# Hybrid decoder step on one core: the first products by two tiles side by side in each chunk, sums of squares and root of x in PSUM

## The chip, the cores and the metric

The kernel runs on one core of a Trainium2 chip. The metric is the device time of one execution in microseconds, the median over several runs. The core has a matrix engine (TensorE; PE, with PEld for its weight loads), VectorE (DVE), ScalarE (ACT), GpSimd (POOL) and a queue, SP, that issues the transfers. Each engine works through its own instructions in the order in which the program issues them.

## The reference, cut to what matters

```
h = RMSNorm(x)                      # x: 1024 prompt + 8 decode rows, 1024 features
parts = h @ w_in                    # q, k, v of 3 dilated groups and one window group, two SiLU gates z, two merge gates g
y = x + W_out( sig(g_A) * (DilAttn(h) * silu(z_A)) @ P_A + sig(g_B) * (SWA(h) * silu(z_B)) @ P_B )
```

All is float32. A product in full precision is made of three products of rounded halves (hi and lo parts): hi by hi, hi by lo and lo by hi. The change lies in how x is normalised and in the first four of the 82 weight tiles, which belong to the merge gates g.

## The kernel before

The 1032 rows lie along the free dimension in three chunks of 344 columns; the 1024 features are eight tiles of 128 (index k). A weight tile is 1024 by 128. `dense_ops` lists the 24 matmuls of a weight tile and a chunk: for each k the products wh·hi, wh·lo, wl·hi. The tiles follow each other in the fixed list `ORDER`, and from tile 4 on a loop (`slot`) issues them, three chunks each, with the attention work of other engines hung between the parts of a slot. The order is written out by hand and nothing moves it.

The opening, lines 1281 to 1345, does tiles 0 to 3 (ga0, gb0, ga1, gb1) while x and the first weights arrive. Chunk 0 is multiplied unnormalised (`h_raw`: hi on ScalarE, line 202, lo on VectorE, line 203); its products are kept (`ev_raw`) and multiplied by the root later (`scale`, line 1267, on GpSimd). Chunks 1 and 2 are normalised first. `squares(j)` squares the eight tiles of chunk j on ScalarE (line 206) and sums them on VectorE into two running sums in SBUF (lines 210 and 212). `h_root(j)` sums over partitions with one float32 matmul (line 216), then takes three ScalarE steps (`rsqrt_act`) and two VectorE steps (lines 241 and 246); the root goes to an SBUF tile `roots[j]`. `h_scale(j, k)` multiplies x by gain and root on VectorE (line 226), rounds hi on ScalarE (line 227) and takes lo = x − hi on GpSimd, for k of 1 and 5 on VectorE (line 232). Later chunk 0 too is scaled so (`scales(0)`), over its raw hi and lo, for tile 4 on.

`w_conv(n)` splits a weight tile: hi on ScalarE (line 137), lo by one GpSimd instruction over all eight k (line 138; tile 0 in two halves). `mm(n, ch, i0, root)` issues 24 matmuls of one tile and, ahead of the one numbered `i0`, `h_root(root)`. Tiles 0 and 1 have PSUM tag "d" (2 buffers), tiles 2 and 3 tag "o" (3); the roots' matmuls have tag "w" (3). `conv_consts` converts small constants on VectorE (lines 1231 to 1236) between the first two and the last six k of `scales(0)`.

Of the kernel before, what the change touches and what calls it, by code (L numbers as in the profile page):

```python
# [10 lines left out]
F32 = mybir.dt.float32  # L11
# [3 lines left out]
ALU = mybir.AluOpType  # L15
# [4 lines left out]
D = 1024  # L20
# [3 lines left out]
KK = D // 128  # L24
CH = 344
# [10 lines left out]
def tile_order():  # L36

    g = [(k, 0, d) for d in range(8) for k in ("ga", "gb")]

    def gates(n):  # L40
        return [g.pop(0) for _ in range(n)]

    GB, GA = (2, 1, 2, 1), ((0, 1, 1), (0, 0, 1), (0, 0, 1), (0, 0, 1))
    o = gates(4) + [("k", 3, 0), ("v", 3, 0), ("q", 3, 0)]
    for c in range(4):
        o += gates(GB[c])
        if c < 3:
            o += [("q", 3, c + 1)]
    for c in range(4):
        for x in range(3):  # L50
            o += [("q", x, c), ("k", x, c), ("v", x, c)] + gates(GA[c][x])
    o += gates(len(g))
    o += [("zb", 0, c) for c in range(4)]
    o += [("za", 0, c) for c in range(4)]
    o += [("br", 0, d) for d in range(8)]
    o += [("out", 0, d) for d in range(8)]
    return o


ORDER = tile_order()  # L60
# [11 lines left out]
def hybrid_step(ctx: ExitStack, tc: tile.TileContext, a):  # L72
    nc = tc.nc
# [11 lines left out]
    def psum(tag, bufs, dt=F32, name=None):  # L85
        return ps.tile([128, 512], dt, tag=tag, bufs=bufs, name=name or "ps_" + tag)
# [38 lines left out]
    def w_load(n, s=None, ks=slice(0, KK)):  # L125
        if n < NT_ALL:
            if n not in stage:
                stage[n] = wp.tile([128, KK, 128], F32, tag="ws", bufs=2, name="w_st") if s is None else s
            nc.sync.dma_start(stage[n][:, ks], a["w"][n][:, ks])

    def w_conv(n, pair=None, ks=slice(0, KK), eng=nc.gpsimd):
        if n < NT_ALL:
            if n not in W:
                W[n] = pair or [wp.tile([128, KK, 128], F32R, tag=t, bufs=2, name="w") for t in ("wh", "wl")]
            s = stage[n][:, ks]
            wh, wl = [w[:, ks] for w in W[n]]
            nc.scalar.activation(wh, s, AF.Copy)  # L137
            eng.tensor_tensor(wl, s, wh.bitcast(F32), op=ALU.subtract)  # L138


    def cache_copies():
# [25 lines left out]
    def ft(name):  # L167
        return bp.tile([128, TT], F32, tag="B", bufs=19, name=name)
# [3 lines left out]
    def tmp(tag, shape, dt=F32, bufs=1):  # L172
        return ap2.tile(shape, dt, tag=tag, bufs=bufs, name=tag)
# [10 lines left out]
    def room(t, n, c0=0):  # L184
        return [t[:, c0 + i * CH:c0 + (i + 1) * CH] for i in range(n)]


    cf, root = ft("cf"), ft("root")
    ones, blk_f = cf[:, 0:128], cf[:, 128:256]
    roots = [root[:, :CH], tmp("rn", [128, CH], bufs=2), tmp("rn", [128, CH], bufs=2)]  # L190
    sq = [room(ft("xsq"), 3) + room(ft("xsq"), 3) + room(root, 2, CH), room(cf, 2, 256)]
    for _ in range(2):
        sq[1] += room(tmp("dkv", [128, 8, 128], bufs=2).rearrange("p k e -> p (k e)"), 2)
    sq[1] += room(tmp("sc", [128, 3, 256], bufs=2).rearrange("p g c -> p (g c)"), 2)
# [1 line left out]
    def sv(j, k):  # L196
        return sq[min(j, 1)][k]
# [7 lines left out]
    def h_square(j, k):  # L205
        nc.scalar.activation(sv(j, k), xs[k][:, cols(j)], AF.Square)

    def h_add(j, k):
        if k > 1:
            nc.vector.tensor_tensor(sv(j, k % 2), sv(j, k % 2), sv(j, k), op=ALU.add)  # L210
        if k == KK - 1:
            nc.vector.tensor_tensor(sv(j, 0), sv(j, 0), sv(j, 1), op=ALU.add)

    def h_root(j):
        pm = psum("w", 3)
        nc.tensor.matmul(pm[:, :CH], ones, sv(j, 0), start=True, stop=True)
        t = tmp("sq", [128, CH])
        rsqrt_act(roots[j], t, pm[:, :CH], D)
        rsqrt_dve(roots[j], t, pm[:, :CH], D)

    late = []

    def h_scale(j, k):
        c = cols(j)
        x = xs[k][:, c]
        nc.vector.scalar_tensor_tensor(x, x, gain[:, k:k + 1], roots[j], op0=ALU.mult, op1=ALU.mult)  # L226
        nc.scalar.activation(hi[:, k, c], x, AF.Copy)
        late.append(k)
        while late and (late[0] < k or k == KK - 1):
            i = late.pop(0)  # L230
            eng = nc.vector if i % 4 == 1 else nc.gpsimd
            eng.tensor_tensor(lo[:, i, c], xs[i][:, c], hi[:, i, c].bitcast(F32), op=ALU.subtract)  # L232

    def rsqrt_act(r, t, ssq, n):

        nc.scalar.activation(r, ssq, AF.Ln, scale=1.0 / n, bias=eps)
        nc.scalar.activation(r, r, AF.Exp, scale=-0.5)  # L237
        nc.scalar.activation(t, r, AF.Square)  # L238

    def newton(t, ssq, n):  # L240
        nc.vector.scalar_tensor_tensor(ssq, ssq, n * EPS, t, op0=ALU.add, op1=ALU.mult)  # L241

    def rsqrt_dve(r, t, ssq, n):

        newton(t, ssq, n)
        nc.vector.scalar_tensor_tensor(r, ssq, -3.0 * n, r, op0=ALU.add, op1=ALU.mult)


    def dense_ops(pt, n, ch, ks, src):
        wh, wl = W[n]  # L250
        s_hi, s_lo = src
        c = slice(ch * CH, (ch + 1) * CH)
        ops = []
        for k, sk in ks:
            ops += [(wh[:, k], s_hi(sk)[:, c]), (wh[:, k], s_lo(sk)[:, c]), (wl[:, k], s_hi(sk)[:, c])]
        N = len(ops)

        def one(i):
            nc.tensor.matmul(pt[:, :CH], ops[i][0], ops[i][1], start=(i == 0), stop=(i == N - 1))  # L259

        return [lambda i=i: one(i) for i in range(N)]
# [862 lines left out]
        else:  # L1124
            after(1, split, True)

    def ev_g(kind, d, ch, pt):
        t = tmp(("sq", "rt", "rn")[ch], [128, CH], bufs=2 if ch == 2 else 1)
        nc.scalar.activation(t, pt[:, :CH], AF.Copy)
        nc.sync.dma_start(g_dr[kind, d][:, ch * CH:(ch + 1) * CH], t)  # L1130

# [39 lines left out]
    H = (lambda k: hi[:, k], lambda k: lo[:, k])  # L1171
# [58 lines left out]
    def conv_consts():  # L1230
        nc.vector.tensor_copy(blk, blk_f)
        nc.vector.tensor_copy(hsel, blk_f[:, ::64])
        nc.vector.tensor_scalar(qkg, qkg, -1.0 / 128, None, op0=ALU.mult)
        for g in range(4):
            nc.vector.tensor_scalar(qg[:, 4 * g:4 * g + 4], slope[:, 0, 4 * (g // 3):4 * (g // 3) + 4], qkg[:, 2 * g:2 * g + 1], None, op0=ALU.mult)
        nc.vector.tensor_scalar(nsink, psink, -1.0, None, op0=ALU.mult)

    def load_tabs():
        tf = ft("tab_f")
        nc.sync.dma_start(tf[:, :256], a["tab"][:, 0])  # L1240
        nc.sync.dma_start(tf[:, 256:384], a["tab3"][:, 0])
        after(4, lambda: nc.vector.tensor_scalar(tabs, tf[:, :384], 1 / slope_of(0), None, op0=ALU.mult))


    NW = 4
# [4 lines left out]
    def mm(n, ch, i0=0, root=None):  # L1250
        pt = psum(*(("o", 3) if n > 1 else ("d", 2)))
        for i, f in enumerate(dense_ops(pt, n, ch, [(k, k) for k in range(KK)], H)):
            if i == i0 and root is not None:
                h_root(root)
            f()
        if ch:
            return lambda: ev_g(ORDER[n][0], ORDER[n][2], ch, pt)
        return lambda: ev_raw(n, pt)

    raws = []  # L1260

    def ev_raw(n, pt):
        t = tmp("P", [128, 512], bufs=3)[:, :CH] if n else tmp("sqh", [128, CH], F32R).bitcast(F32)
        nc.scalar.activation(t, pt[:, :CH], AF.Copy)

        def scale():
            nc.gpsimd.tensor_tensor(t, t, roots[0], op=ALU.mult)
            nc.sync.dma_start(g_dr[ORDER[n][0], ORDER[n][2]][:, :CH], t)

        raws.append(scale)  # L1270

    def squares(j):
        for k in range(KK):
            h_square(j, k)
            h_add(j, k)

    def scales(j, ks=range(KK)):
        for k in ks:
            h_scale(j, k)
# [11 lines left out]
    h_raw(0, 0)  # L1291
    h_raw(0, 1)
    w_conv(0, ks=slice(4, KK))
    h_raw(0, 2)
    h_raw(0, 3)
    w_conv(1)
    w_load(2)
    x_load(1)
# [6 lines left out]
    squares(1)  # L1305
    w_conv(3, [wide(rt("w")) for _ in range(2)])
    w_load(NW)
    e = [mm(0, 0), mm(1, 0)]
    e[0]()
    e += [mm(2, 0, 6, 1)]  # L1310
    e[1]()
    e += [mm(3, 0)]
    scales(1, range(4))
    e[2]()
    scales(1, range(4, KK))
    e[3]()
    squares(0)
    squares(2)
    e = [mm(0, 1), mm(1, 1, 20, 0)]
    e[0]()  # L1320
    e += [mm(2, 1, 16, 2)]
    e[1]()
    scales(2, range(4))
    e += [mm(3, 1)]
    e[2]()
    scales(2, range(4, KK))
    for f in raws:
        f()
    e += [mm(0, 2)]
    e[3]()  # L1330
    scales(0, range(2))
    w_conv(NW)
    e += [mm(1, 2)]
    e[4]()
    w_load(NW + 1)
    conv_consts()
    scales(0, range(2, KK))
    e += [mm(2, 2)]
    e[5]()
    e += [mm(3, 2)]  # L1340
    e[6]()
    e[7]()
    load_tabs()
    for n in range(NW, NT_ALL):
        for ch in range(NCH):
# [125 lines left out]
```

## Time and profile before

| | |
|---|---|
| time, 3 runs | 1206.59 us median (1206.06 to 1210.92) |
| profiled execution | 1207.71 us, its span 1205.9 us |
| matmul engine busy | 1169.6 us (97%) |
| VectorE, ScalarE, GpSimd busy | 689.8, 718.8, 580.7 us |
| opening: first matmul, first of tile 4 | 5.29 us, 70.83 us |
| mean granted clock of TensorE | 0.990 |

The span runs from the first to the last instruction on the profiled chip; the execution's own time is 1.8 us more. Times in the views are microseconds from the start of the span unless ns is written. An arrow and a name behind a row say what ended the idle time ahead of it.

### The profile page before, as it was taken

Reading aid. Unit: us, or ns where it says so; the run is one execution under the profiler, and the core shown is the slowest. Engines: PE = TensorE matmul, PEld = TensorE weight load, DVE = VectorE, ACT = ScalarE, POOL = GpSimd, SP = SyncE. Lnnn points to the kernel's source line nnn. Section 1 sums busy time; section 2 is a strip of 40 time slices with the busy share of each in tenths; the row PEclk is TensorE's granted clock in tenths of the full one; section 3 lists DMA queues with packets and bytes.
Section 4 is the critical chain, followed back from the end, with each engine's and each line's share of the span. In section 5 each row is a group of like instructions: output and inputs, shape, how many; then the busy total and the mean of one; then the engine's idle time right before and its main releaser. Section 6 shows DMA issues by size and latency. Waiting matters only on the chain.

```text
span 1205.9 us, 21988 instructions
## 1 busy us (share of the span) xinstructions
PE 1169.6 (97%) x7689; PEld 1148.6 (95%) x7689; DVE 689.8 (57%) x1700; ACT 718.8 (60%) x1782; POOL 580.7 (48%) x713
## 2 busy tenths in 40 slices
PE   7899999999999999989999899999999989999998
PEld 6799999999999999989999799998999989999998
DVE  5853454576757575766656766768755473333111
ACT  5645566777868685758768587766776423433010
POOL 4453334344425454656455664537544495544220
PEclk9999999999999999989999999999999999999999
DMA  7036665576774869686787679687799566342442
GB/s 232 30 100 190 226 201 189 197 243 199 232 226 165 232 216 293 193 245 175 238 221 247 194 228 257 189 233 199 216 280 252 195 187 232 106 158 89 135 137 98
DMA packets 127135, 237.47 MB, mean 197 GB/s; under 512 B 28632, under 2 KB 102448, under 8 KB 125616
## 3 DMA queue, kind: packets, MB, share of 16 engines
q1 hardware_dynamic: 127024, 236.06, 63.9%
q8 instruction: 61, 1.00, 0.4%
q14 instruction: 50, 0.41, 0.1%
HBM read 178.76 MB, written 113.25 MB: 242 GB/s over the span
## 4 chain that ended last, share of the span: by engine, by line
PE 88%; DVE 5%; DMA 3%; issue 2%; ACT 1%; POOL 1%; SPq 0%; DVEq 0%; POOLq 0%
PE ps_d L259 67%; PE ps_w L259 4%; PE ps_w L512 3%; PE ps_o L582 2%; DMA sc<-sc_dr 2%; PE ps_w L460 2%; PE ps_w L459 2%; PE ps_o L943 1%; PE ps_o L944 1%; PE ps_o L550 1%; PE ps_o L259 1%; PE ps_w L398 1%; PE ps_w L445 1%; DVE dpr L904 1%; DVE x L226 1%
## 5 line engine op out<-in xcount | busy, mean ns | idle before, releaser
L259 PE MATMUL ps_d<-h_hi,w 128*128 128x344 f32 x3456 | 859.0, 324 | 12.2 <-ACT h_hi L202 6.0
L259 PEld LDWEIGHTS ps_d<-h_hi,w 128*128 128x128 f32 x3456 | 604.1, 190 | 16.4 <-ACT h_hi L202 6.8
L259 PE MATMUL ps_d<-h_lo,w 128*128 128x344 f32 x1728 | 569.0, 329 | 5.7 <-POOL h_lo L232 3.1
L259 PEld LDWEIGHTS ps_d<-h_lo,w 128*128 128x128 f32 x1728 | 328.7, 190 | 10.5 <-POOL h_lo L232 5.7
L138 POOL TENSOR_TENSOR w<-w_st,w 128x512 fp32r<-128x512 f32 (+1 forms) x159 | 210.8, 1328 | 179.2 <-ACT w L137 160.3
L478 ACT ACTIVATE P<-P,st 128x256 f32<-128x256 f32 (+1 forms) x256 | 115.9, 454 | 69.5 <-DVE st L468 58.3
L137 ACT ACTIVATE w<-w_st 128x512 fp32r<-128x512 f32 (+1 forms) x160 | 100.2, 630 | 67.0 <-PE ps_d L259 59.8
L949 POOL TENSOR_TENSOR qn<-qn,rn 128x344 f32<-128x344 f32 x48 | 45.4, 945 | 142.2 <-ACT rn L237 125.8
L536 DVE TENSOR_TENSOR pt<-ps_w,pt 128x384 fp32r<-128x384 f32 (+1 forms) x112 | 49.4, 441 | 56.6 <-ACT pt L535 56.3
L535 ACT ACTIVATE pt<-ps_w 128x384 fp32r<-128x384 f32 (+1 forms) x112 | 44.2, 395 | 53.3 <-DVE pt L536 42.2
L949 POOL TENSOR_TENSOR kn<-kn,rn 128x344 f32<-128x344 f32 x39 | 36.6, 938 | 62.2 <-ACT rn L237 55.4
L934 ACT ACTIVATE sq<-ps_d 128x344 f32<-128x344 f32 x87 | 39.5, 454 | 42.3 <-PE ps_d L259 40.2
L512 PE MATMUL ps_w<-ident,P 128*128 128x128 f32 x400 | 61.8, 272 | 1.5 <-DVE pt L536 1.5
L785 POOL TENSOR_TENSOR dkv<-dkv,qb 128x512 f32<-128x512 f32 x32 | 42.2, 1327 | 31.7 <-DMA dkv<-in_ca 18.4
L1167 DVE TENSOR_TENSOR xres<-ps_d,xres 128x344 f32<-128x344 f32 x24 | 12.4, 517 | 76.1 <-PE ps_d L259 45.8
L939 DVE TENSOR_TENSOR sql<-sq,sqh 128x344 fp32r<-128x344 f32 x87 | 54.6, 627 | 1.0
L241 DVE SCALAR_TENSOR_TENSOR ps_o<-ps_o,rt 128x344 f32<-128x344 f32 x87 | 45.2, 519 | 17.1 <-ACT rt L238 16.9
L512 PEld LDWEIGHTS ps_w<-ident,P 128*128 128x128 f32 x400 | 50.4, 140 | 3.8 <-issue 2.0
L460 PE MATMUL ps_w<-k_b,q_st 128*128 128x128 f32 (+1 forms) x192 | 52.0, 282 | 0.0
L335 POOL TENSOR_TENSOR q_st<-qn,q_hi 128x512 fp32r<-128x512 f32 x32 | 45.1, 1428 | 11.0 <-ACT q_hi L334 10.4
L468 DVE CUSTOM_DVE_ANT_0 P<-ps_w,tab 128x256 f32<-128x256 f32 (+1 forms) x128 | 43.4, 375 | 11.4 <-PE ps_w L460 11.3
L938 ACT ACTIVATE sqh<-sq 128x344 fp32r<-128x344 f32 x87 | 42.8, 492 | 11.5 <-PE ps_o L943 9.1
(227 smaller groups left out, 2020.4 us busy)
## 6 DMA issues: line engine op xcount, KB each, us to landing
w_st<-in_w SPq DMA_DIRECT2D x81, 512.0 KB
out_sa<-in_ca SPq DMA_DIRECT2D x16, 1020.0 KB
dkv<-in_ca SPq DMA_DIRECT2D x24, 512.0 KB
q_st<-q_hi SPq DMA_DIRECT2D x32, 256.0 KB
k_st<-k_st SPq DMA_DIRECT2D x48, 128.0 KB
sc<-sc_dr SPq DMA_DIRECT2D x32, 192.0 KB
k_a<-k_b SPq DMA_DIRECT2D x18, 256.0 KB
k_b<-k_a SPq DMA_DIRECT2D x18, 256.0 KB
```

Of the source, the lines that this page charges most:

```text
L137: nc.scalar.activation(wh, s, AF.Copy)
L138: eng.tensor_tensor(wl, s, wh.bitcast(F32), op=ALU.subtract)
L241: nc.vector.scalar_tensor_tensor(ssq, ssq, n * EPS, t, op0=ALU.add, op1=ALU.mult)
L259: nc.tensor.matmul(pt[:, :CH], ops[i][0], ops[i][1], start=(i == 0), stop=(i == N - 1))
L335: nc.gpsimd.tensor_tensor(j.view_o(q1[:, :T])[:, c], v, h.bitcast(F32), op=ALU.subtract)
L460: nc.tensor.matmul(pt[:, o:o + 128 * nk], j.sq[h][:, q], j.sk[h][:, k], start=False, stop=True)
L478: nc.scalar.activation(u.p[:, c], u.p[:, c], AF.Exp, scale=-1.0, bias=st[:, qb, h:h + 1], accum_out=st[:, qb, 2 + h:3 + h])
L512: nc.tensor.transpose(pt[:, o:o + 128], u.p[:, o:o + 128], ident)
L535: nc.scalar.activation(t[:, p0:p0 + m], pt[:, o:o + m], AF.Copy)
L536: nc.vector.tensor_tensor(t[:, 512 + p0:512 + p0 + m], pt[:, o:o + m], t[:, p0:p0 + m].bitcast(F32), op=ALU.subtract)
L939: after(0, lambda: nc.vector.tensor_tensor(sl, s, sh.bitcast(F32), op=ALU.subtract))
L949: nc.gpsimd.tensor_tensor(dst[:, col], dst[:, col], r, op=ALU.mult)
```

## The change

Four edits, all in the opening. (1) `pair(ch)` issues tiles 0 and 1 of a chunk side by side, alternating by k: three matmuls of tile 1, three of tile 0; in chunk 0 the first twelve of tile 0 come ahead. (2) The squares are summed into one running sum in PSUM (`roots[j]`, tag "w"; the last add goes to SBUF), and the root ends in that same PSUM buffer, where `h_scale` reads it; the raw products of chunk 0 are scaled on VectorE in place of GpSimd. (3) For tiles 0 to 3 the lo weights made on GpSimd are made by four instructions per call. (4) `conv_consts` goes behind all of `scales(0)`, `squares(2)` ahead of `squares(0)`, the root of chunk 1 goes from matmul 6 to 12 of tile 2, that of chunk 0 from matmul 20 of tile 1 to matmul 20 of tile 3 in chunk 1 (behind the first half of `scales(2)`), that of chunk 2 from 16 to 18 of tile 2; the outputs of tiles 0 to 2 for chunks 1 and 2 get two tiles of their own (`gst`) in place of the shared ones.

```diff
             nc.scalar.activation(wh, s, AF.Copy)
-            eng.tensor_tensor(wl, s, wh.bitcast(F32), op=ALU.subtract)
+            m = s.shape[1] // 4 if n < NW and eng is nc.gpsimd else s.shape[1]
+            for k in range(0, s.shape[1], m):
+                eng.tensor_tensor(wl[:, k:k + m], s[:, k:k + m], wh[:, k:k + m].bitcast(F32), op=ALU.subtract)
...
-    cf, root = ft("cf"), ft("root")
+    cf = ft("cf")
-    roots = [root[:, :CH], tmp("rn", [128, CH], bufs=2), tmp("rn", [128, CH], bufs=2)]
-    sq = [room(ft("xsq"), 3) + room(ft("xsq"), 3) + room(root, 2, CH), room(cf, 2, 256)]
+    roots = {}
+    sq = [room(ft("xsq"), 3) + room(ft("xsq"), 3) + room(ft("xsq"), 2), room(cf, 2, 256)]
...
     def h_add(j, k):
-        if k > 1:
-            nc.vector.tensor_tensor(sv(j, k % 2), sv(j, k % 2), sv(j, k), op=ALU.add)
-        if k == KK - 1:
-            nc.vector.tensor_tensor(sv(j, 0), sv(j, 0), sv(j, 1), op=ALU.add)
+        if k == 0:
+            roots[j] = psum("w", 3)[:, :CH]
+        else:
+            acc = roots[j]
+            nc.vector.tensor_tensor(acc if k < KK - 1 else sv(j, 0), acc if k > 1 else sv(j, 0), sv(j, k), op=ALU.add)
 
     def h_root(j):
-        pm = psum("w", 3)
-        nc.tensor.matmul(pm[:, :CH], ones, sv(j, 0), start=True, stop=True)
+        pm = roots[j]
+        nc.tensor.matmul(pm, ones, sv(j, 0), start=True, stop=True)
         t = tmp("sq", [128, CH])
-        rsqrt_act(roots[j], t, pm[:, :CH], D)
-        rsqrt_dve(roots[j], t, pm[:, :CH], D)
+        r = tmp("rn", [128, CH], bufs=2)
+        rsqrt_act(r, t, pm, D)
+
+        newton(t, pm, D)
+        nc.vector.scalar_tensor_tensor(pm, pm, -3.0 * D, r, op0=ALU.add, op1=ALU.mult)
...
-        if ch:
-            return lambda: ev_g(ORDER[n][0], ORDER[n][2], ch, pt)
-        return lambda: ev_raw(n, pt)
+        return lambda: ev_first(n, ch, pt)
+
+    outs = {}
+
+    def ev_first(n, ch, pt):
+        if ch == 0:
+            ev_raw(n, pt)
+            return
+        if n == 0:
+            outs[ch] = ft("gst")
+        ev_g(ORDER[n][0], ORDER[n][2], ch, pt, outs[ch][:, n * CH:(n + 1) * CH] if n < 3 else None)
+
+    def pair(ch):
+
+        pt = [psum("d", 2) for _ in range(2)]
+        ops = [dense_ops(p, n, ch, [(k, k) for k in range(KK)], H) for n, p in enumerate(pt)]
+        late = 0 if ch else 12
+        for f in ops[0][:late]:
+            f()
+        for i in range(0, 24, 3):
+            for f in ops[1][i:i + 3] + ops[0][late + i:late + i + 3]:
+                f()
+        return [lambda n=n: ev_first(n, ch, pt[n]) for n in range(2)]
...
-            nc.gpsimd.tensor_tensor(t, t, roots[0], op=ALU.mult)
+            nc.vector.tensor_tensor(t, roots[0], t, op=ALU.mult)
...
```

The opening's order behind `w_load(NW)`, as it is after the change:

```
for f in pair(0): f()
e2 = mm(2, 0, 12, 1); scales(1, range(4)); e3 = mm(3, 0); e2(); scales(1, range(4, KK)); e3()
squares(2); squares(0)
e0, e1 = pair(1); e0(); e1()
e2 = mm(2, 1, 18, 2); scales(2, range(4)); e3 = mm(3, 1, 20, 0); e2(); scales(2, range(4, KK))
for f in raws: f()
e0, e1 = pair(2); e3(); scales(0, range(2)); w_conv(NW); e0(); e1()
w_load(NW + 1); scales(0, range(2, KK))
e2 = mm(2, 2); e3 = mm(3, 2); e2(); e3()
conv_consts(); load_tabs()
```

## Rows read from the trace of the kernel before

**Rows 1.** Page of the profile: part 1, then part 4 by line.

```profile
PE 1169.6 (97%) x7689; PEld 1148.6 (95%) x7689; DVE 689.8 (57%) x1700; ACT 718.8 (60%) x1782; POOL 580.7 (48%) x713
...
PE ps_d L259 67%; PE ps_w L259 4%; PE ps_w L512 3%; PE ps_o L582 2%; DMA sc<-sc_dr 2%; PE ps_w L460 2%; PE ps_w L459 2%; PE ps_o L943 1%; PE ps_o L944 1%; PE ps_o L550 1%; PE ps_o L259 1%; PE ps_w L398 1%; PE ps_w L445 1%; DVE dpr L904 1%; DVE x L226 1%
```

**Rows 2.** Windows by stage: length, busy (count) by engine, PEclk, DMA share, GB/s.

```profile
5.29:21.53 16.24, 12.94 (x48) 10.22 (x49) 11.51 (x15) 10.71 (x20) 7.45 (x4) 1.00 1.04 342
21.53:29.68 8.15, 8.15 (x52) 7.95 (x51) 4.66 (x7) 3.35 (x7) 3.44 (x3) 1.00 0.27 83
29.68:40.95 11.27, 9.69 (x53) 7.89 (x52) 9.20 (x17) 8.66 (x23) 4.41 (x4) 1.00 0.00 0
40.95:49.06 8.11, 8.11 (x51) 7.91 (x51) 5.80 (x12) 5.46 (x12) 0.89 (x1) 1.00 0.13 45
49.06:63.25 14.19, 12.08 (x50) 9.84 (x49) 14.08 (x17) 5.09 (x12) 12.24 (x12) 0.76 0.28 92
63.25:70.83 7.58, 7.58 (x50) 7.58 (x49) 6.38 (x9) 3.64 (x8) 5.49 (x6) 1.00 0.18 63
```

**Rows 3.** TensorE's timeline, opening: start, length, instruction, count, [idle before].

```profile
13.94 0.66 PE L259 MATMUL ps_d<-h_lo,w 128*128 128x344 f32 x1 [1.50 <-DVE h_lo L203]
...
17.33 0.42 PE L259 MATMUL ps_d<-h_lo,w 128*128 128x344 f32 x1 [0.45 <-DVE h_lo L203]
...
52.67 0.43 PE L259 MATMUL ps_d<-h_lo,w 128*128 128x344 f32 x1 [0.80 <-POOL h_lo L232]
...
57.55 0.78 PE L259 MATMUL ps_d<-h_hi,w 128*128 128x344 f32 x2
...
60.99 0.69 PE L259 MATMUL ps_d<-h_hi,w 128*128 128x344 f32 x2
```

**Rows 4.** Chain of waits, opening: start, length, what.

```profile
10.20 1.06 ACT w L137
...
22.63 0.59 PE ps_w L216 x2
```

**Rows 5.** Timeline of VectorE, opening.

```profile
11.76 5.52 DVE L203 SCALAR_TENSOR_TENSOR h_lo<-x,gain,h_hi 128x344 fp32r<-128x344 f32 x4 [2.04 <-ACT h_hi L202]
...
25.99 1.55 DVE L226 SCALAR_TENSOR_TENSOR x<-x,gain,rn 128x344 f32<-128x344 f32 x3
27.61 1.09 DVE L232 TENSOR_TENSOR h_lo<-x,h_hi 128x344 fp32r<-128x344 f32 x1
28.62 3.39 DVE L226 SCALAR_TENSOR_TENSOR x<-x,gain,rn 128x344 f32<-128x344 f32 x4
...
56.20 0.93 DVE L1231 CAST blk<-cf 128x128 fp32r<-128x128 f32 x1
...
61.39 2.44 DVE L1236 TENSOR_SCALAR nsink<-psink 128x8 f32<-128x8 f32 x1
```

**Rows 6.** Timeline of GpSimd, opening.

```profile
11.33 2.18 POOL L138 TENSOR_TENSOR w<-w_st,w 128x1024 fp32r<-128x1024 f32 x1 [2.47 <-ACT w L137]
...
34.94 0.92 POOL L232 TENSOR_TENSOR h_lo<-x,h_hi 128x344 fp32r<-128x344 f32 x1 [0.97 <-ACT h_hi L227]
```

**Rows 7.** Line 138, whole run: ns as min/median/max, first and last start.

```profile
L138 POOL TENSOR_TENSOR w<-w_st,w x159: 1252/1291/2753, 7.6 to 1181.7; 128x512 fp32r<-128x512 f32 x155, 128x1024 fp32r<-128x1024 f32 x4
```

**Rows 8.** Timeline of ScalarE, opening.

```profile
35.11 2.38 ACT L206 ACTIVATE xsq<-x 128x344 f32<-128x344 f32 x6
...
41.20 0.54 ACT L236 ACTIVATE root<-ps_w,eps 128x344 f32<-128x344 f32 x1
```

**Rows 9.** Lines 226, 953, 1115, whole run: the same columns.

```profile
L226 DVE SCALAR_TENSOR_TENSOR x<-x,gain,rn x16: 561/574/1248, 26.0 to 54.1; 128x344 f32<-128x344 f32 x16
...
L953 DVE SCALAR_TENSOR_TENSOR kn<-ps_o,kn x39: 516/517/519, 81.7 to 878.3; 128x344 f32<-128x344 f32 x39
...
L1115 DVE TENSOR_TENSOR sq<-sq,ps_d x24: 491/514/514, 922.9 to 1021.8; 128x344 f32<-128x344 f32 x24
```

**Rows 10.** Tile sc, whole run: idle us before its transfer, times.

```profile
  DMA sc<-sc_dr: 23.9, 8
```

More of the change, by code (lines that the diff above doesn't have):

```diff
@@ L241, in newton @@
         nc.vector.scalar_tensor_tensor(ssq, ssq, n * EPS, t, op0=ALU.add, op1=ALU.mult)
-    def rsqrt_dve(r, t, ssq, n):
-        newton(t, ssq, n)
-        nc.vector.scalar_tensor_tensor(r, ssq, -3.0 * n, r, op0=ALU.add, op1=ALU.mult)
     def dense_ops(pt, n, ch, ks, src):
@@ L1125, in ev_z, with ev_g @@
             after(1, split, True)
-    def ev_g(kind, d, ch, pt):
-        t = tmp(("sq", "rt", "rn")[ch], [128, CH], bufs=2 if ch == 2 else 1)
+    def ev_g(kind, d, ch, pt, t=None):
+        if t is None:
+            t = tmp(("sq", "rt", "rn")[ch], [128, CH], bufs=2 if ch == 2 else 1)
         nc.scalar.activation(t, pt[:, :CH], AF.Copy)
@@ L1307, in hybrid_step @@
     w_load(NW)
[L1308 to L1312, printed above, removed]
+    for f in pair(0):
+        f()
+    e2 = mm(2, 0, 12, 1)
     scales(1, range(4))
-    e[2]()
+    e3 = mm(3, 0)
+    e2()
     scales(1, range(4, KK))
-    e[3]()
+    e3()
+    squares(2)
     squares(0)
[L1318 to L1322, printed above, removed]
+    e0, e1 = pair(1)
+    e0()
+    e1()
+    e2 = mm(2, 1, 18, 2)
     scales(2, range(4))
-    e += [mm(3, 1)]
-    e[2]()
+    e3 = mm(3, 1, 20, 0)
+    e2()
     scales(2, range(4, KK))
@@ L1328, in hybrid_step @@
         f()
-    e += [mm(0, 2)]
-    e[3]()
+    e0, e1 = pair(2)
+    e3()
     scales(0, range(2))
     w_conv(NW)
-    e += [mm(1, 2)]
-    e[4]()
+    e0()
+    e1()
     w_load(NW + 1)
-    conv_consts()
[L1337 to L1342, printed above, removed]
+    scales(0, range(2, KK))
+    e2 = mm(2, 2)
+    e3 = mm(3, 2)
+    e2()
+    e3()
+    conv_consts()
     load_tabs()
```

## Prediction

> **What bounds the kernel now.** I read the page first: TensorE is busy for 97% of the span and its products of line 259 make up two thirds of the chain that ended last [rows 1]. So only what lengthens TensorE's own stream counts, and I looked where that stream has holes. The table by stage shows them in the opening, the only place that the change touches: twelve tile-chunks, 288 products, from 5.29 to 70.83 us [rows 2]. The last stage is what a pair of tiles costs undisturbed: 48 products in 7.58 us, 0.158 each. Against that the first pair took 16.24 us, the pair of chunk 1 11.27 us, the pair of chunk 2 14.19 us; the two pairs in between (8.15 and 8.11) carry one root each, so a root's matmul costs some 0.55, and so does the one hidden in the 11.27. TensorE's timeline says what the rest is. First, its clock: at its lower level (1.2 GHz) twelve products take 57.55 to 60.99, 0.287 each, and the granted clock of that stage is 0.76 [rows 2, 3]. It ran so until 17.33 (the same product is 0.66 long at 13.94 and 0.42 at 17.33, whatever the clock's column says of that stage), and again from about 54.5 to 61.2. Second, waits for lo and hi parts of x, 0.45 to 1.50 us apiece in the rows shown [rows 3].
>
> Then I asked what the parts wait for. In the first pair VectorE needs 5.52 us for four lo parts while GpSimd holds two weight conversions of over 2 us [rows 5, 6]. In the scaling of a chunk, three multiplications by the root take 1.55 us as long as GpSimd rests and four take 3.39 once it makes lo parts [rows 5]. Each multiplication takes either about 0.57 or up to 1.25 us [rows 9].
>
> **Part 1: the first pair.** The removed waits are those for k of 4 to 7. Twelve products of tile 0 end at about 10.9 as before or a little earlier. Then tile 1 must have its weights: hi is done at 11.26 [rows 4]; this is unchanged, and 36 products are left. The next gate is the first lo piece. No row shows a 128x256 GpSimd instruction; its price lies between a quarter of the 1024 one (0.55) and the 128x344 one (0.92) [rows 6]; I take 0.72, on the line through the 344 and the 512 (1.29) [rows 6, 7]. It ends near 12.05 and costs TensorE some 0.25. From there VectorE's lo parts and the pieces take turns (0.57 and 0.72), so lo parts 4 to 7 come at about 12.6, 13.9, 15.1 and 16.4, while TensorE, with six products of 0.287 per k, asks for them at 12.7, 14.4, 16.1 and 17.8: no wait. The clock: before, TensorE worked nearly unbroken from 13.94 and ran at the upper level from 17.33 [rows 3]. I keep 17.33; unbroken work that starts at 12.1 could bring it earlier (0.8 us of gain per 1.6 us), not later. So 5.8 us at 0.287 make 20 products, 16 at 0.158 take 2.5, and tile 2 starts at 19.8 in place of 21.53: **1.7 saved**. The four pieces of tiles 2 and 3 add 0.7 each to GpSimd (4 × 0.72 against 2.18); they end by 19.4 and 22.8, ahead of tile 3 at 24.2, so that is hidden; without the cover it would be 1.4.
>
> **Part 2: sums and root in PSUM.** The seven adds were 0.45 apart in SBUF; a VectorE instruction that has to wait for the one before it in PSUM goes at about 0.55, so a chain costs 3.9 in place of 3.2. In chunk 1 it ends at about 20.4, before TensorE reaches the root at 19.8 + 12 × 0.158 = 21.7: hidden, else 0.7. From the root's matmul to the first multiplication took 25.99 − 22.47 (0.16 before the row shown) = 3.5 and still does: the first multiplication of `scales(1)` starts at 25.2 [rows 4, 5].
>
> What a multiplication costs with the root in PSUM the trace doesn't show in this exact form. Bounds: blocked as now, chunk 1's scaling lasts from 25.99 to 35.86, 9.9 us [rows 5, 6]; never blocked, 0.52 each. The nearest rows have one tensor in SBUF and one in PSUM, and both are steady with GpSimd at work beside them: 516 to 519 ns at line 953, 491 to 514 at line 1115 [rows 9]. I take 0.53. Only the two lo parts on VectorE still queue behind GpSimd (1.09 [rows 5]). By hand: 25.2, multiplications at 0.53, lo 1 at 27.2 to 27.7 behind GpSimd's lo 0, lo 5 at 31.1, the last lo part at 33.2, 8.0 us in all. The Trainium skill ("SBUF — State Buffer", section "SBUF: two separate sides") says that VectorE and GpSimd share a port pair as an exclusive lock, taken by a VectorE instruction with two SBUF inputs; the rows agree as far as they go. By it as it stands the sum is the one below; should the gain's column count as a second SBUF input, by it some 3.6 us are saved, the third rival.
>
> The pair of chunk 1 starts at 19.8 + 7.58 + 0.55 = 27.9 and, side by side, wants a new k only every 0.95 us: lo 7 is asked for at 34.7 and there at 33.2. **No wait is left: 11.27 becomes 7.6** and the pair ends at 35.5; its root moves to the next stage.
>
> **Part 3: the roots of chunks 2 and 0.** ScalarE does 16 squares (0.38 apart [rows 8]) from 32.7 to 38.8, then two outputs and the root of chunk 2; `scales(2)` starts at about 42.3. TensorE does tile 2 (root 2), tile 3 (root 0) to 35.5 + 7.58 + 1.1 = 44.2. Here the new order costs something. The root of chunk 0 stands on ScalarE and VectorE between the two halves of `scales(2)`. Its three ScalarE steps (1.55, like those of root 1) stand behind hi 3 (45.95), its two VectorE steps (1.1) behind those, and the fifth multiplication behind these: 48.6 in place of 45.4. So hi 4 comes at 49.7 and lo 4 at 50.6. TensorE has k of 0 to 3 from 44.2 to 48.0, then waits 1.7, does one product, waits 0.9; the other 23 end at 54.2. **A wait of 2.6 us takes the place of those removed.**
>
> **The clock there.** Before, it fell after TensorE had waited several times between 50.8 and 53.9, nearly 2 us in all, and rose after unbroken work from 57.10 to 61.2 [rows 2, 3]. A hole of 2.6 us is likelier than not to do the same. Unbroken work of 3.4 to 4.1 us at half rate costs half of it, 1.7 to 2.0. I count 1.8: the pair ends at 56.0.
>
> **Part 4: the rest.** Tiles 2 and 3 of chunk 2 take 7.58, so tile 4 starts at **63.6** against 70.83: 7.2 saved. Chunk 0 must be scaled by then. VectorE scales the four raw products (4 × 0.53) from 52.0, then the eight x; with the weight conversion of tile 4 on GpSimd (2.4) in between, lo 7 is ready at about 64 and wanted at 66.9. Hidden by 3 us, by 1 without the clock's fall. `conv_consts` took from 56.20 to 63.83 behind busy GpSimd [rows 5]; now it runs from 61 to 68.7 at worst, wanted by the first output of tile 4 at 67.4, whose buffer isn't needed before 71: hidden. The new output tiles take ScalarE's wait for an earlier transfer away, off TensorE's path: nothing. From tile 4 on the order is the same and TensorE is the bound, so what is saved stays saved.
>
> **Sum**, stage by stage: −1.7 (first pair, 16.24 to 14.5), 0 (8.15 stays), −3.7 (chunk 1's pair, 11.27 to 7.6), +0.6 (8.11 to 8.7, the second root), −2.4 (chunk 2's pair, 14.19 to 11.8), 0 (7.58 stays): −7.2 us. The profiled execution's 1207.71 gives 1200.5; it lies 1.1 above the median of 1206.59, so I forecast **1199.4**.
>
> **The rivals.**
> - The clock does not fall in chunk 2's pair (22%): tile 4 starts at 61.8, 9.0 saved, 1197.6. For it: chunk 1's pair had some 2.4 us of waits spread over 7 us and kept its clock at 1.00 [rows 2]. Against: the hole is denser now.
> - It falls for twice as long, as it did from 54.5 to 61.2 (10%): 1.8 more, 1201.2. For it: that row; against: no second wait is due after 50.6.
> - Multiplications stay blocked by GpSimd (15%): scaling takes 9.9, 1.9 more per chunk. The delay in chunk 1 is handed on through the squares to the start of `scales(2)`, so its last lo part comes 3.8 later, at 56.9, and chunk 2's pair ends at 57.8 in place of 54.2: 3.6 us of the gain are gone, 1203.0. For it: x and gain are both in SBUF; against: line 953.
> - No measurable change (4%): the lo pieces, or the two products interleaved, are waited for as whole tiles; tile 1 then stands until 15.9 and the first pair ends some 1 us later than before, and the ScalarE order eats the rest; about 1205.
> - Slower (4%), by one mechanism outside the opening: the attention part waits 23.9 us in 8 places for score transfers [rows 10]. Their issue keeps its place in the order, but if the earlier start packed the queue so that each wait grew, 7.2 us would be gone at 0.9 each and 6 us of loss would be reached at 1.65 each: 1213. Against: weights, copies and scores all move together with TensorE's stream.
> - The forecast itself: 45%.
>
> **How the numbers follow.** Within 0.5% (6 us) is about what a measurement can't tell from no change, so faster starts below 1200.6. The forecast case spreads by some 1.5 us around 1199.4 (first rise of the clock, later stalls that meet the clock otherwise), four fifths of it below; nearly all of the second case, a third of the third and a tenth of the fourth too: 0.36 + 0.21 + 0.03 + 0.01 = 0.61. Slower 0.04; same 0.35. The range, 1196.3 to 1203.5, leaves out the last two cases and the edges of the others.
>
> **What would show it.** Tile 2's first product near 19.8, chunk 1's pair in about 7.6 us without a wait, multiplications by the root at a steady 0.53 beside GpSimd, a hole near 48 to 50.6 with ScalarE's root of chunk 0 ahead of it, and tile 4 near 63.6. Wrong would be the forecast if tile 1 waited for all four lo pieces, if line 226 kept two durations, or if the stream behind tile 4 lengthened.

## The result, and the profile after

The changed kernel takes 1199.22 us, median of 12 runs (1197.04 to 1205.71); the kernel before, in 12 runs, 1207.29 (1204.97 to 1213.02). The ratio is 0.9942, with a 95% interval of 0.9930 to 0.9954: 5.6 to 8.5 us saved, 7.0 in the middle; the two medians lie 8.1 us apart. The forecast was 7.2 saved and 1199.4. The profiled execution took 1199.29 us with a span of 1197.5.

The stages of the opening after the change, cut at the first product of the same tiles as in [rows 2] (length, busy time and count of PE, PEld, DVE, ACT, POOL, granted clock, DMA share, GB/s):

```profile
5.22:19.39 14.17, 12.98 (x48) 10.67 (x49) 9.45 (x15) 9.49 (x19) 8.82 (x12) 1.00 1.01 330
19.39:27.57 8.18, 8.18 (x53) 7.98 (x51) 4.41 (x9) 4.47 (x9) 4.37 (x6) 1.00 0.62 192
27.57:35.12 7.55, 7.55 (x51) 7.55 (x49) 5.36 (x10) 6.01 (x16) 4.42 (x5) 1.00 0.00 1
35.12:43.80 8.68, 8.68 (x53) 8.28 (x53) 7.66 (x16) 6.05 (x15) 0.37 (x1) 1.00 0.12 42
43.80:54.12 10.32, 8.37 (x50) 7.56 (x49) 8.10 (x16) 5.79 (x14) 5.73 (x7) 1.00 0.21 75
54.12:61.70 7.58, 7.58 (x50) 7.58 (x49) 7.04 (x14) 4.63 (x11) 7.08 (x7) 1.00 0.54 178
```

Against [rows 2] the first pair takes 14.17 for 16.24, chunk 1's pair 7.55 for 11.27, chunk 2's pair 10.32 for 14.19, and the stage with two roots 8.68 for 8.11. Tile 4 starts at 61.70 in place of 70.83: 9.1 us earlier. Chunk 1's pair is without a wait, at the price of the undisturbed pair (7.55 against 7.58). In chunk 2's pair the granted clock reads 1.00 where it was 0.76.

VectorE's timeline, after (start, length, instruction, count), the rows that answer to [rows 5]:

```profile
12.10 3.37 DVE L205 SCALAR_TENSOR_TENSOR h_lo<-x,gain,h_hi 128x344 fp32r<-128x344 f32 x4 [2.33 <-ACT h_hi L204]
...
24.81 1.54 DVE L232 SCALAR_TENSOR_TENSOR x<-x,gain,ps_w 128x344 f32<-128x344 f32 x3
26.42 0.86 DVE L238 TENSOR_TENSOR h_lo<-x,h_hi 128x344 fp32r<-128x344 f32 x1
27.21 2.01 DVE L232 SCALAR_TENSOR_TENSOR x<-x,gain,ps_w 128x344 f32<-128x344 f32 x4
...
37.56 3.04 DVE L215 TENSOR_TENSOR ps_w<-ps_w,xsq 128x344 f32<-128x344 f32 x5
40.71 0.52 DVE L215 TENSOR_TENSOR xsq<-ps_w,xsq 128x344 f32<-128x344 f32 x1
```

The four raw lo parts take 3.37 us for 5.52, four multiplications by the root 2.01 for 3.39. Over the whole run the multiplication has one duration now (min/median/max ns, first and last start):

```profile
L232 DVE SCALAR_TENSOR_TENSOR x<-x,gain,ps_w x24: 555/558/573, 24.8 to 58.1; 128x344 f32<-128x344 f32 x24
```

555 to 573 ns, with GpSimd at work beside it or not, where [rows 9] had 561 to 1248. What is left in chunk 2's pair, beside 0.28 us of wait at its first lo part, is one hole: TensorE loses 1.25 us ahead of the first and 0.85 ahead of the second of these rows, 2.1 in all. TensorE's timeline, after:

```profile
49.38 0.43 PE L260 MATMUL ps_d<-h_hi,w 128*128 128x344 f32 x1 [1.09 <-ACT h_hi L233]
50.39 0.42 PE L260 MATMUL ps_d<-h_lo,w 128*128 128x344 f32 x1 [0.58 <-POOL h_lo L238]
```

The chain of waits tells what stands in it (start, length, what):

```profile
45.24 0.49 ACT h_hi L233
45.73 0.45 ACT rn L242
46.20 0.50 ACT rn L243
46.73 0.50 ACT sq L244
47.23 0.02 issue
47.25 0.54 DVE ps_w L247
47.81 0.52 DVE ps_w L225
48.33 0.48 DVE x L232
48.84 0.50 ACT h_hi L233
49.34 0.07 issue
49.41 0.94 POOL h_lo L238
```

That is the forecast's chain, step by step: hi 3, three ScalarE steps and two VectorE steps of chunk 0's root, the fifth multiplication, hi 4, lo 4. It was put at 48.0 to 50.6; it is there from 48.1 to 50.4.

### The profile page after: what moved, and what is told of

It reads as the page before. It is cut to its first block, busy times and chain, and to the rows that moved or that the text cites. A ratio compares the mean times of both kernels' runs of the same rounds, so it can differ in the third digit from the quotient of the medians.

```text
span 1197.5 us, 22006 instructions
## 1 busy us (share of the span) xinstructions
PE 1164.6 (97%) x7689; PEld 1146.8 (96%) x7689; DVE 680.4 (57%) x1704; ACT 717.9 (60%) x1782; POOL 577.3 (48%) x721
## 4 chain that ended last, share of the span: by engine, by line
PE 87%; DVE 5%; DMA 3%; ACT 2%; issue 2%; POOL 1%; SPq 0%; DVEq 0%; POOLq 0%; ACTq 0%
PE ps_d L260 66%; PE ps_w L260 4%; PE ps_w L513 3%; PE ps_o L583 2%; DMA sc<-sc_dr 2%; PE ps_w L460 2%; PE ps_w L461 2%; PE ps_o L944 1%; PE ps_o L551 1%; PE ps_o L945 1%; PE ps_o L260 1%; PE ps_w L399 1%; DVE dpr L905 1%; PE ps_w L446 1%; DMA q_st<-q_st 1%
## 5 line engine op out<-in xcount | busy, mean ns | idle before, releaser
L140 POOL TENSOR_TENSOR w<-w_st,w 128x512 fp32r<-128x512 f32 (+2 forms) x171 | 213.6, 1254 | 175.0 <-ACT w L137 154.2
L247 DVE SCALAR_TENSOR_TENSOR ps_o<-ps_o,rt 128x344 f32<-128x344 f32 x87 | 45.2, 519 | 16.9 <-ACT rt L244 16.5
L460 PE MATMUL ps_w<-k_a,q_st 128*128 128x128 f32 (+1 forms) x192 | 49.7, 282 | 0.7 <-DMA q_st<-q_st 0.7
L607 DVE TENSOR_TENSOR n_t<-ps_o,ot 64x512 f32<-64x512 f32 x48 | 32.8, 683 | 30.5 <-ACT ot L606 30.5
```

The lines of the kernel that those rows point to most:

```text
L140: eng.tensor_tensor(wl[:, k:k + m], s[:, k:k + m], wh[:, k:k + m].bitcast(F32), op=ALU.subtract)
L460: nc.tensor.matmul(pt[:, o:o + 128 * nk], j.sq[h][:, q], j.ka[h][:, k], start=True, stop=False)
```

## The experiments

There were eleven further runs, two of them of the changed kernel itself. Each of the others differs from the changed kernel by the edit shown. The table takes from the profiles, in us: the first product at the upper clock level ("clock up": the first row of TensorE's timeline with a single product of 0.34 us or less), the first product of tile 2, the way from there to the first of tile 4, and the rest (span less the start of tile 4).

| kernel | ratio to before (95%) | clock up | tile 2 | 2 to 4 | rest |
|---|---|---|---|---|---|
| before | 1 | 17.9 | 21.53 | 49.30 | 1135.1 |
| changed | 0.9942 (0.9930 to 0.9954) | 15.8 | 19.39 | 42.31 | 1135.8 |
| changed, second time | 0.9938 (0.9918 to 0.9958) | 15.4 | 19.01 | 42.32 | 1136.7 |
| changed, third time | 0.9941 (0.9918 to 0.9965) | 12.8 | 17.31 | 42.41 | 1134.6 |
| root in SBUF | 0.9979 (0.9961 to 0.9996) | 16.5 | 19.58 | 46.98 | 1135.5 |
| first pair in turn | 0.9947 (0.9930 to 0.9965) | 16.7 | 19.82 | 42.30 | 1139.2 |
| one lo instruction | 0.9933 (0.9908 to 0.9959) | 17.8 | 20.98 | 42.31 | 1132.6 |
| both edits of chunk 0 undone | 0.9964 (0.9951 to 0.9977) | 19.9 | 22.59 | 43.86 | 1134.8 |
| later pairs in turn | 0.9981 (0.9963 to 0.9999) | 16.8 | 19.93 | 47.73 | 1134.5 |
| constants between | 0.9946 (0.9928 to 0.9963) | 15.4 | 18.56 | 42.30 | 1136.8 |
| chunk 0's root late | 0.9924 (0.9897 to 0.9951) | 14.6 | 18.64 | 40.09 | 1133.9 |
| the same, second time | 0.9917 (0.9904 to 0.9930) | 17.4 | 20.02 | 40.12 | 1135.6 |
| and tile 1's weights in halves | 0.9915 (0.9901 to 0.9929) | 16.7 | 19.34 | 40.14 | 1135.0 |

The column "2 to 4" repeats to 0.11 us in six profiles that have the same order on TensorE there (42.30 to 42.41); tile 2's start and the rest do not repeat so.

**The changed kernel again, twice.** No edit.

> The changed kernel once more, unchanged. Theory (the hole of 2.1 us in chunk 2's pair sometimes meets the clock and sometimes not): tile 4 starts at 61.9 where TensorE's clock stays up and near 63.5 where it falls behind the hole; a mean granted clock of 0.993 goes with the first, 0.991 with the second; ratio to the kernel before 0.993 to 0.995. Rival (the clock never falls there): 61.9 again, and times of 1199 to 1200 come from later stages.

> The changed kernel a third time, to stand beside the next ones on one chip. Theory (the opening saves 9 us, the stream behind tile 4 varies by some us from run to run with its own waits and the clock): tile 4 starts at 61 to 62, the rest lasts between 1133 and 1139 us, ratio to the kernel before 0.992 to 0.995. Rival (something behind tile 4 steadily gives 1 to 2 us back): the rest lasts 1137 or more again.

Tile 4 started at 61.33 and 59.72; the latter is below what was expected, because tile 2 was early. The clock did not fall in chunk 2's hole in any of the three profiles. What it did in the executions without a profile is not recorded, and their mean granted clock does not tell it, as the first expectation had assumed: two profiles below with a mean of 0.991 (first pair in turn, constants between) have the same hole and no fall in it. The three rests were 1134.6 to 1136.7, around the 1135.1 of the one profile of before, so no steady loss behind tile 4 shows; the rival of the second expectation fell. But the rest of all thirteen profiles spans 1132.6 to 1139.2, which is more than most edits are worth. It has waits of its own: in the changed kernel's first profile, TensorE's waits of 3.5, 1.8 and 3.5 us that end at 684, 835 and 988 are three of them, with the clock down behind each. Windows of the changed kernel there:

```profile
670.00:700.00 30.00, 24.97 (x159) 24.22 (x159) 22.72 (x55) 20.54 (x49) 16.35 (x21) 0.94 0.79 246
820.00:850.00 30.00, 26.14 (x169) 25.39 (x168) 25.58 (x50) 16.26 (x40) 17.80 (x24) 0.94 0.81 228
970.00:1000.00 30.00, 24.44 (x144) 23.83 (x143) 21.16 (x23) 7.89 (x18) 25.29 (x29) 0.94 0.51 169
```

In the second profile the first and the last of these windows have a granted clock of 0.89 and 1.00, so what these waits cost differs from run to run. The opening is therefore read from the timelines, the sum from the ratios.

**Root in SBUF.** The sums stay in PSUM.

```diff
-        nc.vector.scalar_tensor_tensor(pm, pm, -3.0 * D, r, op0=ALU.add, op1=ALU.mult)
+        nc.vector.scalar_tensor_tensor(r, pm, -3.0 * D, r, op0=ALU.add, op1=ALU.mult)
+        roots[j] = r
```

> Sums stay in PSUM, but the root is written to SBUF and read from there. Theory (the multiplications by the root wait for GpSimd when their two tensors both lie in SBUF): line of the multiplication goes back to two durations, about 0.57 and up to 1.25 us; a chunk's scaling lasts some 9.9 us in place of 7.8; tile 4 starts at about 65.5 in place of 61.9; the time rises by 3 to 5 us against the changed kernel. Rival (the order did it, not the place of the root): all multiplications near 0.56, tile 4 at 62 to 62.5.

The multiplication in that run (whole run, ns min/median/max), then chunk 2's pair in TensorE's timeline:

```profile
L233 DVE SCALAR_TENSOR_TENSOR x<-x,gain,rn x24: 564/574/2743, 25.0 to 66.8; 128x344 f32<-128x344 f32 x24
```

```profile
52.57 0.42 PE L261 MATMUL ps_d<-h_hi,w 128*128 128x344 f32 x1 [1.54 <-ACT h_hi L234]
53.80 0.66 PE L261 MATMUL ps_d<-h_lo,w 128*128 128x344 f32 x1 [0.81 <-POOL h_lo L239]
```

The waiting multiplications are back (chunk 1's scaling takes 9.9 us, from 24.99 to 34.87), and the way from tile 2 to tile 4 is 4.7 longer; the ratio rose by 0.0041 against the changed kernel measured beside it (0.9938), 4.9 us, and the two intervals do not overlap. The theory holds. The price is near the top of what was expected; in this profile the clock fell in the hole (the second row is 0.66 long, the first 0.42).

**Later pairs in turn.** Chunks 1 and 2 only.

```diff
+        if ch:
+            for f in ops[0] + ops[1]:
+                f()
...
```

> In chunks 1 and 2, tile 1 follows tile 0 as before the change; chunk 0 stays side by side. Theory (side by side halves the pace at which TensorE asks for scaled parts): chunk 1's pair takes about 9.1 us in place of 7.55, chunk 2's about 11.6 in place of 10.3, tile 4 starts near 64.7, and later still by 1.8 if the clock falls; time up by 2.5 to 4.5 us. Rival (with the root in PSUM scaling is quick enough either way): tile 4 at 62 to 62.5.

Windows of chunk 1's and chunk 2's pair in that run, and the longest wait of the second:

```profile
28.10:37.35 9.25, 8.57 (x50) 7.47 (x49) 6.75 (x13) 7.70 (x21) 4.42 (x5) 1.00 0.00 1
46.05:60.11 14.06, 11.18 (x51) 10.25 (x49) 10.37 (x21) 6.82 (x14) 8.12 (x7) 0.76 0.25 89
...
50.83 0.59 PE L260 MATMUL ps_d<-h_hi,w 128*128 128x344 f32 x1 [2.01 <-ACT h_hi L233]
```

Chunk 1's pair takes 9.25, as expected (9.1). Chunk 2's takes 14.06, with the clock down (0.76), and tile 4 comes at 67.66, some 1.2 us later than expected even with a fall. The ratio is 0.0039 above the changed kernel's 0.9942, 4.7 us, and the intervals do not overlap. The quicker scaling alone does not hide the waits: asked for every 0.47 us instead of every 0.95, the parts are late again. The rival fell.

**One lo instruction.**

```diff
-            m = s.shape[1] // 4 if n < NW and eng is nc.gpsimd else s.shape[1]
+            m = s.shape[1]
```

> The lo weights of a call by one GpSimd instruction again; all else as changed. Theory (one long instruction holds VectorE's lo parts off and tile 1's first lo weight is late): VectorE's four lo parts take 5 us or more in place of 3.4, TensorE waits near 12.3 until 13.9, tile 2 starts at 20.8 to 21.2 in place of 19.4, tile 4 near 63.5, time up by 1.3 to 2 us. Rival (four instructions cost GpSimd more than one and gain nothing): tile 2 at 19.4 to 19.8.

VectorE's timeline and TensorE's in that run:

```profile
11.97 5.52 DVE L205 SCALAR_TENSOR_TENSOR h_lo<-x,gain,h_hi 128x344 fp32r<-128x344 f32 x4 [2.36 <-ACT h_hi L204]
```

```profile
13.77 0.94 PE L260 MATMUL ps_d<-h_hi,w 128*128 128x344 f32 x2 [1.31 <-POOL w L140]
```

The lo parts take the 5.52 us of before to the digit [rows 5], TensorE waits for the lo weight until 13.77, and tile 2 starts at 20.98: the opening is as the theory said. The time is not: the ratio, 0.9933, is that of the changed kernel, and this run's rest, 1132.6, is the shortest of all. So the 1.6 us that the pieces are worth at tile 2 in this profile were not resolved in the time, and the expected rise of 1.3 to 2 us did not show.

**The first pair in turn.**

```diff
-        late = 0 if ch else 12
+        late = 0 if ch else 24
```

> In chunk 0 alone, tile 1 follows tile 0 as before the change; lo weights stay in four pieces. Theory (side by side fills the wait for k of 4 to 7 and lets the clock rise sooner): tile 2 starts at 20.5 to 20.9 in place of 19.4, tile 4 at 63.0 to 63.4, the time up by 1 to 1.5 us. Rival (the four pieces alone freed VectorE, the order of the two tiles adds nothing): tile 2 at 19.4 to 19.7, time within 0.3 us.

Tile 2 started at 19.82, sooner than expected and within the spread of kernels with an unchanged first pair (17.31 to 20.02 in the table). The ratio is 0.0009 above that of the changed kernel beside it, 1.1 us, as the theory has it, but well inside both intervals, and this run's rest, 1139.2, is the longest of all. Theory and rival are not told apart.

**Both edits of chunk 0 undone**: the last two edits together.

> Both edits of chunk 0 undone: tile 1 behind tile 0, lo weights by one GpSimd instruction; the rest as changed. Theory (either edit alone is worth little, the two remove the same wait together): tile 2 starts at 21.2 to 21.7 as before the change, tile 4 near 64, time up by 1.5 to 2.5 us against the changed kernel. Rival (the pieces do it all): tile 2 at 21.5 too, so this run tells it apart only together with the run in turn with pieces: there 19.8 would then have to be the pieces' gain alone.

TensorE's timeline in that run:

```profile
17.41 0.65 PE L260 MATMUL ps_d<-h_lo,w 128*128 128x344 f32 x1 [0.47 <-DVE h_lo L205]
...
19.92 0.32 PE L260 MATMUL ps_d<-h_lo,w 128*128 128x344 f32 x1
```

Tile 2 started at 22.59, a microsecond later than before the change: the waits near 14 and 17 are those of [rows 3], but the clock rose at 19.9 and not by 17.9. The ratio rose by 0.0023 against the changed kernel measured beside it, 2.8 us, though the two intervals overlap. In the profile 1.5 us of the way from tile 2 to 4 is the clock, which fell in this run's hole (granted 0.86 for chunk 2's pair) although the hole is no longer than the changed kernel's (1.95 us of wait in chunk 2's pair in both).

By the start of tile 2, the two edits are not told apart: it is at about 20 to 21 with either one, 21.5 to 22.6 with neither, and the clock's moment moves it by more than the difference. The waits say more. They are the length of the first pair less TensorE's busy time, the first two numbers of its window; here without the order, without the pieces, and without both:

```profile
5.21:19.82 14.61, 12.95 (x49) 10.63 (x50) 9.80 (x16) 10.23 (x20) 8.81 (x12) 1.00 1.01 337
...
5.16:20.98 15.82, 13.02 (x48) 11.01 (x49) 11.28 (x15) 10.59 (x20) 6.62 (x4) 1.00 0.99 336
...
5.22:22.59 17.37, 13.64 (x48) 11.19 (x49) 12.11 (x16) 10.72 (x20) 8.21 (x4) 1.00 0.98 324
```

That is 1.7, 2.8 and 3.7 us of wait, where before the change it was 3.3 and the eight profiles with both edits have 0.6 to 1.6. Most of the waiting therefore goes with the pieces, and the theory that either edit alone is worth little does not hold for them; what the order adds is not above the spread of these profiles. In the time, neither edit's part was resolved.

**Constants between.** Edit: `conv_consts()` goes back ahead of the last six k of `scales(0)`.

> The constants are converted between the first two and the last six k of chunk 0's scaling again. Theory (their 4 to 7.5 us on VectorE would now make chunk 0's lo parts late): chunk 0's last lo part moves from 62.5 to 66.5 or later, tile 4's first chunk waits 1.5 us or more, time up by 1.5 to 4 us. Rival (hidden at either place): no wait of TensorE in tile 4's first chunk, time within 0.3 us.

VectorE's timeline in that run:

```profile
52.93 0.21 DVE L1233 CAST blk<-cf 128x128 fp32r<-128x128 f32 x1
...
53.40 1.11 DVE L1237 TENSOR_SCALAR qg<-slope,qkg 128x4 f32<-128x4 f32 x4
54.43 0.15 DVE L1238 TENSOR_SCALAR nsink<-psink 128x8 f32<-128x8 f32 x1
```

The theory fell. The eight instructions took 1.65 us there, with one lo part on GpSimd beside them (53.12 to 54.08). In the changed kernel they run from 58.59 to 62.75, 4.2 us, beside five lo parts in a row; its GpSimd timeline:

```profile
57.76 4.76 POOL L238 TENSOR_TENSOR h_lo<-x,h_hi 128x344 fp32r<-128x344 f32 x5
```

TensorE has no wait in the first 12 us of tile 4 in either, and the way from tile 2 to 4 is 42.30 against the changed kernel's 42.31. No gain from moving the constants last is to be seen.

**Chunk 0's root late, twice.** The matmul stays, its steps go behind `scales(2)`.

```diff
+        if j:
+            h_rsq(j)
+
+    def h_rsq(j):
+        pm = roots[j]
...
     scales(2, range(4, KK))
+    h_rsq(0)
```

> The matmul of chunk 0's root stays at its place, but its three ScalarE and two VectorE steps are issued behind all of chunk 2's scaling, ahead of the raw products. Theory (the hole in chunk 2's pair is the fifth multiplication standing behind that root): the hole from 48.1 to 50.4 is gone but for some 0.3 us at its first lo part, chunk 2's pair takes about 8 us in place of 10.3, tile 4 starts at 59.6 to 60.0, the time falls by about 2 us against the changed kernel. Rival (the hole only moves: chunk 0's scaling is now late for tile 4): chunk 2's pair is short, but tile 4's first chunk waits for lo parts and the time is within 0.5 us of the changed kernel.

> The kernel with chunk 0's root issued behind chunk 2's scaling once more, for its time. Theory: tile 4 at 58.7 to 59.8, 2 us under the changed kernel of the same call, ratio to the kernel before near 0.991. Rival (the rest gives it back): tile 4 as early, but the time within 0.5 us of the changed kernel.

The chain of waits in the first of these runs:

```profile
43.65 7.67 PE ps_d L265 x47
```

47 products without a wait: the hole is gone, and the way from tile 2 to 4 is 40.1 in both runs, 2.2 shorter. Tile 4 started at 58.73 and 60.14, and TensorE waits at most 0.07 us in its first 12, so the hole did not move there. The second time, the ratio is 0.0024 lower than that of the changed kernel measured beside it, 2.9 us, though the two intervals overlap. That the hole is made by chunk 0's root ahead of the fifth multiplication is shown by the profile; the gain in time agrees with it.

**And tile 1's weights in halves**, on top of the last.

```diff
-    w_conv(1)
+    w_conv(1, ks=slice(0, 4))
+    h_raw(0, 4)
+    h_raw(0, 5)
+    w_conv(1, ks=slice(4, KK))
...
-    for k in range(4, KK):
+    for k in range(6, KK):
         h_raw(0, k)
```

Each `w_conv` makes its lo weights by four instructions, so tile 1's are made in eight pieces of one k here, in place of four of two.

> As the kernel with chunk 0's root late, and tile 1's weights are converted in two halves with two raw parts of x between them. Theory (behind the first twelve products TensorE waits for all of tile 1's hi weights, 1.06 us on ScalarE): tile 1's first product starts near 11.2 in place of 11.65, tile 2 up to 0.4 us sooner, tile 4 at 58.3 to 59.4. Rival (the moment at which the clock rises decides, not the first product): tile 2 between 18.6 and 19.9 as in the other runs.

Tile 1's first product started at 11.17 in place of 11.61 in the run above, tile 2 at 19.34, within the spread, and tile 4 at 59.48. The rival holds as far as one run can say. At 1196.94 us, ratio 0.9915, this is the fastest version that ran, 10.3 us under the kernel before (by the interval of the ratio 8.6 to 12.0), and not separable from the one without the halves.

## Why the prediction was right

- *Only TensorE's stream counts, and the opening is where the change can shorten it.* Right: 9.1 us less in the opening, and a rest of 1135.8 after against 1135.1 before.
- *The first pair, 1.7 saved, tile 2 at 19.8.* 2.1 saved in the profile, tile 2 at 19.39 and between 17.3 and 20.0 over the runs. The waits that go are the named ones, for k of 4 to 7. The clock was assumed to rise at 17.33 as before (17.9 by the measure of the table); it rose at 15.8, 15.4 and 12.8 in the three profiles, the early side of what was allowed, and beyond it.
- *A GpSimd piece takes 0.72 and pieces and lo parts take turns.* Four pieces without VectorE beside them took 2.82, 0.70 each. But the four lo parts took 3.37, 0.84 each, and not 0.57 + 0.72. GpSimd did its eight pieces of that time in 6.57, 0.82 each; four lo parts and four pieces strictly by turns would have taken 4 × (0.57 + 0.70) = 5.1, so the turns overlap in part.
- *Multiplications by the root at 0.53, never blocked; scaling 8.0 us.* 0.555 to 0.573; chunk 1's scaling lasts from 24.81 to about 32.6, 7.8. So line 953 was the right neighbour, and the rule of the Trainium skill ("SBUF — State Buffer", section "SBUF: two separate sides"), a lock taken by two SBUF inputs, agrees as it stands: x and the gain's column are both in SBUF, and the column does not count. The run with the root in SBUF, up to 2.74 us for one multiplication, shows it from the other side.
- *The chain of seven adds in PSUM goes at 0.55.* 0.63 apart (five in 3.04, and 40.71 − 37.56 = 3.15 for five steps), 4.4 for a chain and not 3.9. ScalarE's work was what led to the start of `scales(2)` at 42.3; it starts at 42.25, but ScalarE's last step of that root ends at 40.3, and what stands just ahead are VectorE's last adds, for chunk 0, and its two steps of the root. The time was right, the neighbour wrong.
- *Chunk 1's pair without a wait, 7.6; the two-root stage 8.7.* 7.55 and 8.68.
- *A hole of 2.6 us in chunk 2's pair, made by chunk 0's root.* The hole was there, 2.1 long, and moving the root took it away.
- *The clock falls there, 1.8 us.* This step failed in the profiles of the changed kernel: tile 4 at 61.7 is the first rival's 61.8. The same hole fell in one profile of the seven that have it (both edits of chunk 0 undone), and in the two runs with longer holes (root in SBUF, later pairs in turn) it fell. It was a term with a chance, and it came out on the side that was called less likely.
- *The rest stays.* No loss behind tile 4 is shown: the rest of the changed kernel's three profiles is 1134.6 to 1136.7, against 1135.1 in the one profile of before. But the forecast's 7.2 was meant to be all opening. The opening gave 9.1 in the profile (9.5 and 11.1 in the other two, against the same profile of before), while the ratio says 7.0 with 1.4 either way and the two profiled executions lie 8.4 apart. Where the difference goes stays open: the opening of before is known from a single profile, and whether the clock falls in the hole in executions without a profile is not recorded. So the mechanism was right in its waits and the closeness of the sum is in part luck: the opening gained more than forecast, since the clock's 1.8 us did not come, and the whole gained less than the opening.
- *Constants last, raw products on VectorE, own output tiles: nothing.* Borne out for the constants; the others were not tried alone.

## What to carry to other kernels

When two engines share a path to memory, a longer instruction is not the price to look at but the wait that it hands to the other: one operand moved to PSUM made all 24 multiplications steady, and cutting one instruction in four freed the neighbour. Two products side by side halve the pace at which the matrix engine asks for operands; that hides a producer which is slower than one product but faster than two. And with an in-order engine, look at what a moved step stands in front of: chunk 0's root, issued half a chunk ahead of what first needs it, made the one hole that was left.

## What the runs showed of the hardware that was not expected

The moment at which TensorE's clock first rises is not set by the program alone. In three profiles of one kernel whose first products start within 0.03 us of each other (5.19 to 5.22), it rose at 15.8, 15.4 and 12.8, and tile 2 moved from 19.39 to 17.31 with it. The short waits ahead of the rise were not the same in the three (1.2, 0.9 and 0.6 us in the whole first pair); whether they or something outside the program made the difference stays open. The third of these, TensorE's timeline:

```profile
12.13 0.47 PE L260 MATMUL ps_d<-h_lo,w 128*128 128x344 f32 x1
12.42 0.50 PE L260 MATMUL ps_d<-h_hi,w 128*128 128x344 f32 x2
12.76 0.32 PE L260 MATMUL ps_d<-h_lo,w 128*128 128x344 f32 x1
```

against the first:

```profile
15.20 0.76 PE L260 MATMUL ps_d<-h_hi,w 128*128 128x344 f32 x2
15.77 0.34 PE L260 MATMUL ps_d<-h_lo,w 128*128 128x344 f32 x1
```

The Trainium skill ("TensorE: Matmul & The Clock Gate", section "What you observe") puts the run-to-run spread of that moment, for matmuls issued back to back, at half a microsecond either way. Here, with short waits between the products, the three runs differ by 3 us. An edit of the first microseconds that is worth less than the 2.1 us by which tile 2 moved can't be judged from tile 2's start in one profile.
